# Order of strands in the first mixers from an estimate of VectorE's and ScalarE's queues

## The chip, the core and the metric

The kernel runs on one core of a Trainium2 chip. The core has a TensorE (PE in the profile; PEld is its weight load), a VectorE (DVE), a ScalarE (ACT), a GpSimd (POOL) and a SyncE (SP), which here only issues transfers. Each engine works through its own instruction stream in order and waits on semaphores for the others. The metric is the device time of one execution in microseconds.

## The reference

Two transformer blocks on one sequence of 256 tokens of width 1024, in fp32.

```
first_block:   xn = rms_norm(x); proj = xn @ w_in            # 1024 -> 2048 + 1792 columns
               ret = silu(g) * head_norm(retention(rotary(q), rotary(k), v))   # 4 heads of 128
               rw  = rwkv7_time_mix(rest of proj)            # 8 heads of 64, a state updated token by token
               h = x + concat(ret, rw) @ w_out
               h = h + hier_moe(rms_norm(h))                 # 32 experts, top 2
second_block:  moba and differential attention, w_out_2, then a PEER layer of 16384 experts
```

The change touches only the part from `proj` to `concat(ret, rw) @ w_out`: the first mixers.

## The kernel before

The first mixers are `phase_a` (L369). Weights come in units of 128 x 1024 fp32 and are multiplied with three products of reduced-precision parts. `ahead` (L190) makes the parts: a raw unit is loaded from SP's queue (L204, four raw buffers), ScalarE rounds it to a first part (`high`, L211), VectorE subtracts to get the second part (`low`, L218, three buffers), and only then is the next raw unit's load written (`load`). Each `next(ws)` hands out one unit and writes the first part three units and the second part two units ahead of its use. `mm3` (L294) multiplies first x first, first x second, second x first.

Thirty of the units are the input projection's (fourteen feature tiles, which are transposed, of 24 matmuls of 256 columns, and four token-major tiles of four units), eight are the output projection's. `features` (L488) and `feature_tile` (L512) compute the input projection. After a feature tile's matmuls VectorE makes three operations of 256 columns (`fe`, `d`, `ft`, L525 to L529).

All work of the first mixers is cut into strands, Python generators: `row_scales`, four `rwkv` (L563, each a pair of heads, in chunks of 64 tokens), two `ret_turn`, `retention`, two `ret_heads`, `out_weights`, `first_experts` (which starts the load of the expert weights into memory given back by the mixers), `features`, `project_out`. A strand writes some matmuls and the VectorE, ScalarE and GpSimd work on their results, and yields either a condition or a number: the planner's microseconds until its next matmuls should be written. `interleave` (L266) keeps one clock, `self.pe`, which each matmul advances by its columns; it always runs the first strand in the list that is ready, and if none is, sets the clock to the earliest wait. `features` yields 0.0, so it is ready whenever its condition holds. What a strand's answers cost on VectorE or ScalarE is in no clock: it is in the written numbers only.

Some of the numbers in an `rwkv` strand: 2.5 ahead of the products with `sq` and `rk`, 5.0 ahead of those with `bd` and `kd` (made by six VectorE operations, one a reciprocal, L637 to L646), 1.0 and 1.2 between the five levels of `X`, `Z`, `XT` (L707, L715, L716), 1.75 between the chunk states `Sb` (L745), 5.5 from the normalisation (L755 to L762, with two GpSimd steps between) to the last transposes.

Of the kernel before, what the change touches and what calls it, by code (L numbers as in the profile page):

```python
# [10 lines left out]
F32 = mybir.dt.float32  # L11
F32R = mybir.dt.float32r
# [3 lines left out]
AF = mybir.ActivationFunctionType  # L16
OP = mybir.AluOpType
# [142 lines left out]
    return o  # L160


class K:
    def __init__(self, ctx, tc, ins, out, dbg=None):
        self.ctx, self.tc, self.nc, self.i, self.out, self.dbg = ctx, tc, tc.nc, ins, out, dbg or {}
        self.n = 0
        self.pe = 0.0
        self.ps = ctx.enter_context(tc.tile_pool(name="ps", bufs=8, space=PSUM))
        self.cp = ctx.enter_context(tc.tile_pool(name="cp", bufs=1))
        self.hip = ctx.enter_context(tc.tile_pool(name="hip", bufs=4))  # L170
        self.raw = ctx.enter_context(tc.tile_pool(name="raw", bufs=RAW))
        self.lop = ctx.enter_context(tc.tile_pool(name="lop", bufs=LOP))
        self.hx = ExitStack()
        self.early = ExitStack()
# [15 lines left out]
    def ahead(self, srcs, depth=RAW):  # L190


        nc = self.nc
        srcs = iter(srcs)
        loaded, first, parts = deque(), deque(), deque()

        def load():
            s = next(srcs, None)
            if s is not None:
                if callable(s):  # L200
                    loaded.append(s)
                    return
                loaded.append(self.unit(self.raw))
                nc.sync.dma_start(loaded[-1], s)  # L204

        def high():
            if loaded:
                r = loaded.popleft()
                r = r() if callable(r) else r
                hi = self.unit(self.hip, F32R)  # L210
                nc.scalar.activation(hi, r, AF.Copy)  # L211
                first.append((hi, r))

        def low():
            if first:
                hi, r = first.popleft()
                lo = self.unit(self.lop, F32R)
                nc.vector.tensor_tensor(lo, r, hi.bitcast(F32), OP.subtract)  # L218
                parts.append((hi, lo))
                load()  # L220

        for _ in range(depth):
            load()
        yield
        high()
        yield
        low()
        high()
        yield
        low()  # L230
        high()
        yield
        while parts:
            high()
            low()
            yield parts.popleft()

    @staticmethod
    def halves(chunks):
# [22 lines left out]
    def tr(self, out, x):  # L262
        self.pe += 0.06
        self.nc.tensor.transpose(out, x, self.ident)  # L264

    def interleave(self, gens):  # L266

        wait = [0.0] * len(gens)  # L270
        live = dict(enumerate(gens))
        cond = {}
        while live:
            for n in list(cond):
                if cond[n]():
                    del cond[n]
                    wait[n] = self.pe
            ready = [n for n in live if n not in cond and wait[n] <= self.pe]
            if not ready:
                n = min((n for n in live if n not in cond), key=lambda n: wait[n])  # L280
                self.pe = max(self.pe, wait[n])
                ready = [n]
            n = ready[0]
            try:
                d = next(live[n])
            except StopIteration:
                del live[n]
                continue
            if callable(d):
                cond[n] = d  # L290
            else:
                wait[n] = self.pe + d

    def mm3(self, out, lh, rh, start, stop):  # L294
        mm = self.mm
        mm(out, lh[0], rh[0], start=start, stop=False)
        mm(out, lh[0], rh[1], start=False, stop=False)
        mm(out, lh[1], rh[0], start=False, stop=stop)
# [70 lines left out]
    def phase_a(self):  # L369
        nc, tc, i = self.nc, self.tc, self.i  # L370
        with ExitStack() as cx:

            early, even, self.bx = ExitStack(), ExitStack(), ExitStack()
            self.ap = {n: {"first": early, "even": even}.get(n, cx).enter_context(
                           tc.tile_pool(name=f"a_{n}", bufs=1, side="right" if n == "even" else "left"))
                       for n in ("even", "odd", "mid", "end", "xt", "tiny", "late", "first")}
            T = lambda pool, shape, tag, dt=F32, **k: self.t(self.ap[pool], shape, dt, tag, **k)
            lora, gup = (T("first", [128, 512], tag) for tag in ("lora", "gup"))
            nc.gpsimd.dma_start(lora, i["lora"])
            nc.gpsimd.dma_start(gup, i["gup"])  # L380
            rot = T("mid", [128, 2, 2, 64], "rot")
            nc.gpsimd.dma_start(rot, i["rot"])

            xt = [T("xt", [128, 8, S], f"xt{n}_", F32R) for n in range(2)]
            placed = deque()

            def out_weights():
                yield lambda: ("fm", 3) in self.done
                early.close()
                pw = cx.enter_context(tc.tile_pool(name="pw", bufs=1))  # L390
                for k in OUT_ORDER:
                    placed.append(self.t(pw, [128, D], F32, f"wo{k}_"))
                    nc.sync.dma_start(placed[-1], i["wO"][0, k])

            def first_experts():
                yield lambda: ("out", 2) in self.done
                even.close()
                self.places.extend(self.new_place(2 if not n else 1, "right") for n in range(2))
                self.once = ExitStack()
                self.prefetch(self.once.enter_context(tc.tile_pool(name="once", bufs=2, side="right", reuse_waits="tile")))  # L400
                for _ in range(2):
                    self.prefetch()

            self.src = [i["wB"][j] for j in range(192)]
            self.wq = []
            self.places = deque()
            ws = self.ahead(chain(self.halves(i["wA"][j] for j in range(15)), (placed.popleft for k in range(8))))
            self.got, self.done, self.tile = {}, set(), 0
            rt = {"qT": T("late", [128, 2, 4, S], "qT"), "v": T("mid", [128, 2, 512], "vr"), "g": T("late", [128, 2, 512], "gr")}
            rt["rs"] = [self.row_rstd(self.ap["tiny"], self.h[:, t], rt["v" if t else "g"].rearrange("p t d -> p (t d)"), "rows") for t in range(2)]  # L410
            self.transposed([self.h[:, t] for t in range(2)], "norm1_gain", *xt, ws, WARM[1])
            nc.sync.dma_start(self.cst2, i["cst"][:, CST_KEPT:])
            nc.gpsimd.dma_start(self.wr, i["wr"])
            o = VEC["norm2_gain"][0]
            nc.gpsimd.tensor_tensor(self.wr, self.wr, self.vec[:, o:o + 8, None].to_broadcast([128, 8, 36]), OP.mult)
            nc.gpsimd.dma_start(self.br, i["br"].to_broadcast([128, 36]))
            zs = self.rwkv_setup()
            self.interleave([self.row_scales(zs, rt, rot)] + [self.rwkv(p, zs, lora, gup) for p in range(4)] +
                            [self.ret_turn(rot, rt, g) for g in range(2)] +
                            [self.retention(rt)] + [self.ret_heads(rt, n) for n in range(2)] +  # L420
                            [out_weights(), first_experts(), self.features(xt, zs, rt, ws),
                             self.project_out(ws, OUT_ORDER, lambda k: ("ret", k // 2) if k < 4 else ("all", k - 4))])
        self.dump("mixh", self.mix[:, 0].bitcast(F32))
        places = [self.new_place() for _ in PLACES]
        self.places.extendleft(places[n] for n in reversed(PLACES))
        for n in range(3, MR + 3):
            self.prefetch({9: self.raw, 15: self.hip, 16: self.hip}.get(n))
        self.dump("h1", self.h)
# [1441 lines left out]
```

## Time and profile before

| | |
|---|---|
| Median of three runs | 1636.73 us (1633.51 to 1638.0) |
| Profiled execution | 1633.89 us, of which the span 1632.1 us |
| PE busy | 1581.5 us (97%) |
| VectorE busy | 967.6 us (59%) |
| ScalarE busy | 654.9 us (40%) |
| GpSimd busy | 218.8 us (13%) |

Shares over the whole span mix stages with different limits. The first mixers are the first 230 us or so, then come the experts, then the second block. The rows below are read by stretch, by wait and by instruction in time. A busy PE is one with matmuls under way; their ends are modelled, so small pauses can hide in it.

### The profile page before, as it was taken

The numbers are of one execution on the slowest core, as the hardware profiler recorded it, in microseconds if no ns is written. First come the engines' busy times: TensorE is split into PE (matmuls) and PEld (weight loads), VectorE is DVE, ScalarE is ACT, GpSimd is POOL, SyncE is SP. The second block draws the span as 40 slices with busy tenths as digits, with TensorE's granted clock in tenths as the row PEclk, the third lists the DMA queues.
The fourth block names the chain that finished last, engine by engine and source line by source line (L and its number), as shares of the span: only waits on it lengthen the run. The fifth ranks groups of instructions, "written<-read, shape, count | busy, mean of one in ns | idle before, by whom it ended". The sixth has DMA issues, their size and how long they took to land.

```text
span 1632.1 us, 28041 instructions
## 1 busy us (share of the span) xinstructions
PE 1581.5 (97%) x11118; PEld 1217.2 (75%) x11118; DVE 967.6 (59%) x1845; ACT 654.9 (40%) x1171; POOL 218.8 (13%) x249
## 2 busy tenths in 40 slices
PE   8999999999999999899999999999999999999998
PEld 7888873443444334378799999999999888888887
DVE  6676561121212112289889997788999755555554
ACT  5333341211111111266655556555544444444443
POOL 3213020000000000174210000123444000000000
PEclk9999999999999999999999999999999999999999
DMA  6324699999999999853355556555555566666664
GB/s 204 105 66 142 228 353 391 405 414 420 419 419 419 420 419 420 345 181 117 98 197 167 188 178 194 162 164 168 162 164 166 169 193 193 193 193 193 194 193 156
DMA packets 84297, 390.61 MB, mean 239 GB/s; under 512 B 9632, under 2 KB 9776, under 8 KB 63424
## 3 DMA queue, kind: packets, MB, share of 16 engines
q1 hardware_dynamic: 83088, 384.45, 65.6%
q0 software_dynamic: 928, 3.25, 0.5%
q8 instruction: 90, 1.47, 0.4%
q10 hardware_dynamic: 144, 1.05, 0.2%
q14 instruction: 47, 0.39, 0.1%
HBM read 386.62 MB, written 2.10 MB: 238 GB/s over the span
## 4 chain that ended last, share of the span: by engine, by line
PE 53%; DVE 2%; POOL 2%; issue 1%; ACT 0%; ACTq 0%; DVEq 0%; POOLq 0%
PE b L252 53%; POOL rs_r L338 1%; DVE u L218 1%; PE b L264 1%; DVE g L1727 0%; POOL rs_m L336 0%; POOL y L1418 0%; POOL rs_r L1407 0%; DVE oh L1835 0%; ACT s L1451 0%; DVE h L469 0%; DVE u L1684 0%; DVE ss L1405 0%; DVE qz L1430 0%; DVE mx L1447 0%
## 5 line engine op out<-in xcount | busy, mean ns | idle before, releaser
L211 ACT ACTIVATE u<-u 128x1024 fp32r<-128x1024 f32 x334 | 354.1, 1061 | 388.2 <-PE b L252 366.2
L218 DVE TENSOR_TENSOR u<-u,u 128x1024 fp32r<-128x1024 f32 x334 | 412.5, 1236 | 150.1 <-PE b L252 114.5
L252 PE MATMUL b<-mix,u 128*128 128x256 f32 x3456 | 425.6, 281 | 0.0
L252 PEld LDWEIGHTS b<-mix,u 128*128 128x128 f32 x3456 | 411.1, 188 | 0.0
L252 PE MATMUL b<-u,oh 128*128 128x512 f32 x1536 | 350.3, 390 | 2.0 <-ACT oh L1667 2.0
L252 PEld LDWEIGHTS b<-u,oh 128*128 128x128 f32 x1536 | 289.3, 188 | 62.8 <-ACT oh L1667 2.2
L252 PE MATMUL b<-mr,u 128*64 128x512 f32 x944 | 232.3, 595 | 16.2 <-DMA mr<-in_wB 16.0
L252 PEld LDWEIGHTS b<-mr,u 128*64 128x64 f32 x944 | 74.5, 137 | 158.0 <-issue 120.7
L1130 DVE TENSOR_TENSOR hh<-hh,b 128x512 f32<-128x512 f32 x16 | 11.0, 688 | 230.2 <-PE b L252 230.2
L1711 POOL TENSOR_TENSOR g<-g,gelu 128x4 f32<-128x4 f32 (+43 forms) x87 | 94.2, 1083 | 355.2 <-ACT gelu L1710 348.2
L252 PE MATMUL b<-u,xt 128*128 128x512 f32 x480 | 123.4, 407 | 0.8 <-DVE u L218 0.8
L252 PE MATMUL b<-mr,hT 128*64 128x512 f32 x480 | 115.5, 596 | 3.6 <-DVEq L1194 1.8
L252 PEld LDWEIGHTS b<-u,xt 128*128 128x128 f32 x480 | 89.1, 191 | 21.5 <-DVE u L218 1.1
L1175 DVE SCALAR_TENSOR_TENSOR u<-b,sw,u 128x512 fp32r<-128x512 f32 x32 | 23.9, 750 | 127.8 <-ACT u L1174 127.8
L252 PEld LDWEIGHTS b<-mr,hT 128*64 128x64 f32 x480 | 35.6, 137 | 70.9 <-issue 63.3
L1155 ACT ACTIVATE hT<-b 128x512 f32<-128x512 f32 x16 | 9.6, 598 | 160.1 <-PE b L264 160.1
L1668 DVE TENSOR_TENSOR oh<-g,oh 128x512 fp32r<-128x512 f32 x64 | 44.3, 693 | 41.1 <-ACT oh L1667 41.0
L1174 ACT ACTIVATE u<-b,sw 128x512 fp32r<-128x512 f32 x32 | 21.9, 687 | 105.1 <-PE b L252 105.1
L1303 POOL MEMSET qz<- 128x2048 f32 x2 | 3.5, 1800 | 448.8 <-DVEq L1194 448.8
L1727 DVE TENSOR_TENSOR g<-g,b 128x252 f32<-128x252 f32 (+47 forms) x111 | 61.5, 592 | 0.0
L1835 DVE TENSOR_TENSOR oh<-oh,gw 128x512 f16<-128x512 f16 x128 | 54.6, 465 | 0.0
L1129 ACT ACTIVATE hh<-b 128x512 f32<-128x512 f32 x16 | 9.6, 597 | 99.3 <-PE b L252 99.3
(381 smaller groups left out, 1713.7 us busy)
## 6 DMA issues: line engine op xcount, KB each, us to landing
mr<-in_wB SPq DMA_DIRECT2D x160, 1024.0 KB, 15.2
u<-in_down SPq DMA_DIRECT2D x128, 512.0 KB, 3.7
u<-in_up SPq DMA_DIRECT2D x128, 512.0 KB, 4.3
mr<-in_wB SPq DMA_DIRECT2D x36, 512.0 KB, 15.0
u<-in_wA SPq DMA_DIRECT2D x30, 512.0 KB, 3.7
u<-in_wB SPq DMA_DIRECT2D x28, 512.0 KB, 14.4
u<-in_wC SPq DMA_DIRECT2D x24, 512.0 KB, 4.0
u<-in_wQ SPq DMA_DIRECT2D x16, 512.0 KB, 3.6
```

The costliest lines, as they stand in the source:

```text
L211: nc.scalar.activation(hi, r, AF.Copy)
L218: nc.vector.tensor_tensor(lo, r, hi.bitcast(F32), OP.subtract)
L252: self.nc.tensor.matmul(out, l, r, start=start, stop=stop, **k)
L264: self.nc.tensor.transpose(out, x, self.ident)
L338: nc.gpsimd.tensor_tensor(r, m, self.mhalf[:, :width], OP.pow)
L1130: nc.vector.tensor_tensor(self.hh, self.hh, bs[1], OP.mult)
L1174: nc.scalar.activation(yh[:, o], b, AF.Copy, scale=sw)
L1175: nc.vector.scalar_tensor_tensor(yl[:, o], b, sw, yh[:, o].bitcast(F32), op0=OP.mult, op1=OP.subtract)
L1668: nc.vector.tensor_tensor(lo, src, hi.bitcast(F32), OP.subtract)
L1711: nc.gpsimd.tensor_tensor(dst[:, 0:n], dst[:, 0:n], g[:, 0:n], OP.mult)
L1727: nc.vector.tensor_tensor(d, d, s, OP.mult)
L1835: self.nc.vector.tensor_tensor(w[:, :, part].rearrange("p t (k x) -> p t k x", x=2), o[:, :, 0].rearrange("p t (k x) -> p t k x", x=2), se ...
```

## The change

A class `Queues` stands in for the program object while the first mixers' strands are written. It hands back every VectorE, ScalarE and GpSimd call unchanged, and keeps an estimated end for each of these three queues: the later of its last end and 0.25 us after the planner's clock, plus a constant and a price per element. GpSimd's end is kept but not used for waits. After a strand's step that wrote VectorE or ScalarE work, the strand's wait becomes the later of its written number and the estimated end plus 0.1.

The second part of a weight unit is no longer written in its `low` call. It is put on a list of what is owed, and written when the estimated end of VectorE's queue lies behind the clock at a strand's turn, or when a second one becomes owed, or when no finished unit is left. The load of the next raw unit moves with it. Where the strands of the second block use the same functions, nothing changes.

```diff
+class Queues:
+    COST = {"vector": (0.07, 1.04e-3), "scalar": (0.125, 0.91e-3), "gpsimd": (0.45, 2.1e-3)}
...
+    def note(self, e, n):
+        a, b = self.COST[e]
+        self.end[e] = max(self.end[e], self.k.pe + 0.25) + a + b * n
+        if e != "gpsimd":
+            self.last = self.end[e]
...
         def low():
             if first:
                 hi, r = first.popleft()
-                lo = self.unit(self.lop, F32R)
-                nc.vector.tensor_tensor(lo, r, hi.bitcast(F32), OP.subtract)
-                parts.append((hi, lo))
-                load()
+
+                def second():
+                    lo = self.unit(self.lop, F32R)
+                    self.nc.vector.tensor_tensor(lo, r, hi.bitcast(F32), OP.subtract)
+                    parts.append((hi, lo))
+                    load()
+                self.owed.append(second)
+                self.pay(0 if not self.queues else 1)
...
-        while parts:
+        while parts or self.owed:
             high()
             low()
+            if not parts:
+                self.pay()
             yield parts.popleft()
+
+    def pay(self, n=0):
+        while len(self.owed) > n:
+            self.owed.popleft()()
...
+    def modelled(self, gens):
+        nc = self.nc
+        self.nc = self.queues = Queues(self)
+        self.interleave(gens)
+        self.nc, self.queues = nc, None
+        self.pay()
...
             n = ready[0]
+            qs = self.queues
+            if qs:
+                qs.last = 0.0
+                if self.owed and qs.end["vector"] <= self.pe:
+                    self.pay(len(self.owed) - 1)
+                    qs.last = 0.0
...
                 wait[n] = self.pe + d
+                if qs and qs.last:
+                    wait[n] = max(wait[n], qs.last + 0.1)
...
-            self.interleave([self.row_scales(zs, rt, rot)] + [self.rwkv(p, zs, lora, gup) for p in range(4)] +
+            self.modelled([self.row_scales(zs, rt, rot)] + [self.rwkv(p, zs, lora, gup) for p in range(4)] +
```

## Rows read from the trace of the kernel before

**Rows 1.** Busy time by stretch: span, then PE, PEld, DVE, ACT, POOL; granted clock; DMA share.

```profile
20.00:60.00 40.00, 38.13 (x431) 33.50 (x429) 37.17 (x74) 18.51 (x35) 9.34 (x13) 1.00 0.41 131
...
100.00:150.00 50.00, 46.00 (x630) 38.76 (x632) 39.77 (x85) 16.49 (x35) 10.38 (x13) 0.93 0.23 75
```

**Rows 2.** The same view, two stretches of the expert stage.

```profile
380.00:400.00 20.00, 19.81 (x103) 9.16 (x101) 5.56 (x11) 4.02 (x9) 0.00 (x0) 1.00 1.01 422
660.00:680.00 20.00, 17.00 (x80) 6.70 (x78) 3.39 (x7) 1.48 (x3) 0.00 (x0) 1.00 0.99 401
```

**Rows 3.** What PE waits for, 10 to 240 us: total us, times, longest us.

```profile
PE b L252 <- DVE Z L707: 3.4, 3, 2.6
PE b L252 <- issue: 2.3, 3, 1.7
PE b L252 <- DVE u L218: 1.7, 1, 1.7
PE b L252 <- DVE Sb L745: 1.4, 1, 1.4
```

**Rows 4.** PE's instructions in time: start, us, what; idle time before and its releaser.

```profile
13.93 2.18 PE L252 MATMUL b<-xt,u 128*128 128x256 f32 x16 [1.74 <-DVE u L218]
...
23.00 0.67 PE L252 MATMUL b<-gs,gup 128*128 128x256 f32 x2 [1.68 <-issue]
...
101.84 1.12 PE L252 MATMUL b<-XT,Z 64*64 64x64 f32 x16 [2.63 <-DVE Z L707]
...
121.14 0.33 PE L252 MATMUL b<-Sb,G 64*64 64x64 f32 x4 [1.43 <-DVE Sb L745]
...
137.30 0.33 PE L252 MATMUL b<-Z,XT 64*64 64x64 f32 x4 [0.60 <-DVE Z L707]
```

**Rows 5.** Busy time by stretch, columns as in rows 1, behind the longest wait.

```profile
101.00:109.00 8.00, 7.16 (x62) 6.42 (x63) 4.34 (x9) 2.34 (x4) 0.00 (x0) 0.57 0.40 133
```

**Rows 6.** Groups by line, first 240 us: count | busy, mean ns | idle before.

```profile
L218 DVE TENSOR_TENSOR u<-u,u 128x1024 fp32r<-128x1024 f32 x30 | 38.2, 1272 | 2.6 <-PE b L252 2.1 <-ACT u L211 0.5
L211 ACT ACTIVATE u<-u 128x1024 fp32r<-128x1024 f32 x30 | 31.6, 1058 | 21.4 <-PE b L252 18.7 <-ACT XT L716 1.7 <-DMA u<-in_wA 0.9
```

**Rows 7.** VectorE's instructions in time around 100 us, columns as in rows 4.

```profile
93.74 0.42 DVE L755 TENSOR_REDUCE s<-b 128x4 f32<-128x256 f32 x1 [0.99 <-PE b L252]
...
95.56 0.42 DVE L760 TENSOR_REDUCE s<-y 128x4 f32<-128x256 f32 x1 [0.73 <-POOL y L759]
97.43 0.43 DVE L762 TENSOR_TENSOR y<-y,rs_r 128x256 f32<-128x256 f32 x1 [1.45 <-POOL rs_r L338]
...
100.15 1.21 DVE L218 TENSOR_TENSOR u<-u,u 128x1024 fp32r<-128x1024 f32 x1
101.28 0.41 DVE L707 TENSOR_TENSOR Z<-b,cst 128x256 f32<-128x256 f32 x1
```

**Rows 8.** VectorE's instructions in time around 120 us.

```profile
115.95 1.22 DVE L218 TENSOR_TENSOR u<-u,u 128x1024 fp32r<-128x1024 f32 x1
...
117.54 1.75 DVE L638 RECIPROCAL ri<-ri 128x256 f32<-128x256 f32 x1
...
120.81 0.28 DVE L745 TENSOR_SCALAR Sb<-b,gam 128x64 f32<-128x64 f32 x1
```

**Rows 9.** Instructions of VectorE and PE in time, 31 to 40 us, and one at 113.

```profile
31.04 0.81 DVE L628 TENSOR_SCALAR k<-av,vec 128x256 f32<-128x256 f32 x1
32.75 1.71 DVE L218 TENSOR_TENSOR u<-u,u 128x1024 fp32r<-128x1024 f32 x1
32.89 0.70 PE L252 MATMUL b<-rk,cst 128*128 128x256 f32 x2 [0.15 <-DVE rk L631]
...
37.68 0.42 DVE L646 TENSOR_TENSOR bd<-kr,e 128x256 f32<-128x256 f32 x1
...
39.27 1.09 PE L252 MATMUL b<-ar,bd 64*64 64x128 f32 x16
...
113.21 0.34 DVE L628 TENSOR_SCALAR k<-av,vec 128x256 f32<-128x256 f32 x1
```

More of the change, by code (lines that the diff above doesn't have):

```diff
@@ L160, in layout, with __init__, __getattr__, noted @@
     return o
+class Counted:
+    def __init__(self, engine, note):
+        self.engine, self.note = engine, note
+    def __getattr__(self, name):
+        f = getattr(self.engine, name)
+        if name == "dma_start":
+            return f
+        def noted(*a, **k):
+            r = f(*a, **k)
+            n = 1
+            for x in (a[1] if name == "tensor_reduce" else a[0]).shape[1:]:
+                n *= x
+            self.note(n)
+            return r
+        return noted
+class Queues:
+    COST = {"vector": (0.07, 1.04e-3), "scalar": (0.125, 0.91e-3), "gpsimd": (0.45, 2.1e-3)}
+    def __init__(self, k):
+        self.k, self.nc = k, k.nc
+        self.end = {e: k.pe for e in self.COST}
+        self.last = 0.0
+        for e in self.COST:
+            setattr(self, e, Counted(getattr(k.nc, e), lambda n, e=e: self.note(e, n)))
+    def __getattr__(self, name):
+        return getattr(self.nc, name)
+    def note(self, e, n):
[3 more added lines that the diff above has]
+            self.last = self.end[e]
 class K:
@@ L167, in __init__ @@
         self.pe = 0.0
+        self.owed, self.queues = deque(), None
         self.ps = ctx.enter_context(tc.tile_pool(name="ps", bufs=8, space=PSUM))
@@ L210, in high @@
                 hi = self.unit(self.hip, F32R)
-                nc.scalar.activation(hi, r, AF.Copy)
+                self.nc.scalar.activation(hi, r, AF.Copy)
                 first.append((hi, r))
```

## The prediction

> **What bounds the kernel now.** I read the stages first. Until 230 us the kernel computes its first mixers, the only part that the change rewrites; PE is busy 38.13 of 40 us in the stretch that starts at 20 us and 46.00 of 50 in the one that starts at 100 [rows 1]. VectorE is busy 37.17 of 40 us in the first of them: it is a near second limit there, and a source of single late answers afterwards. Behind 240 us comes an expert stage in which the DMA engines are full, 1.01 at 380 us and 0.99 at 660 us [rows 2]; its buffers are parts of memory that the first mixers give back, so I take a shift of the first mixers as a shift of the whole, one for one. There is no second effect to look for behind 240 us.
>
> Next, the list of what PE waits for inside the first mixers [rows 3]: VectorE's Z 3.4 us in three waits, its Sb 1.4 us, its second part of a weight ("u L218") 1.7 us, and "issue" 2.3 us. The 1.7 us is one wait that ends at 13.93, before the strands' first answers [rows 4], and the 0.8 us for "sel" that the view also lists belongs to the expert stage. What is left is about 7.8 us: 3.4 + 2.3 + 1.4 and 0.7 in single waits of 0.1 to 0.3. The long ones are 1.68 at 23.00, 2.63 at 101.84, 1.43 at 121.14 and 0.60 at 137.30 [rows 4]. Behind the longest, between 101 and 109 us, the granted clock is 0.57 [rows 5]: nearly all of the stretch ran at 1.2 instead of 2.4 GHz. The low share is 2 x 0.43 = 0.86 of 8 us, 6.9 us, and half of it, 3.4 us, is work that full clock would have saved. So no order of the strands can bring more than about 7.8 + 3.4 = 11.2 us, 0.7%. A measurement of this kernel can tell about 0.3%, 4.9 us, from no change.
>
> **The change part by part.** *The second parts move.* Thirty weight units go through the subtraction at 1272 ns each and eight more through the same line [rows 6]. Nothing is added or removed: the same instruction is written later in VectorE's stream. It helps where it stood ahead of an answer PE waited for. At 100.15 a second part stands directly ahead of the Z at 101.28 [rows 7]: 1.13 us. At 115.95 one stands ahead of the chain with the reciprocal, ahead of the Sb at 120.81 [rows 8]: 1.2 us, of a wait of 1.43. Bounds for both together: 0, if the estimate calls the queue empty and pays anyway, to 4.1, if both waits go (2.63 + 1.43). For the first I take 1.1. The wait at 23.00 is for gs, made from the second feature tile; between these first tiles the estimate finds VectorE's queue empty and pays at once, so I leave it (bound: 1.2 saved).
>
> What could be late in its place is the second part itself: at most one unit, 24 matmuls or some 3 us later. From 14 us on PE never waits for one, with two finished units in hand; one stays in hand. I cost it at nothing; with VectorE behind as it is from 20 to 60 us, the cover could fail once or twice at 1.2 us each (bounds 0 to 3). The load of the next raw unit is written with the second part, so SP's issue also comes up to a unit later, and the weight loads, the output weights and the expert prefetch behind it on that queue move with it. ScalarE waited for a weight's landing 0.9 us in all [rows 6]; I cost it at nothing, with the raw units in hand as cover, and bounds 0 to 2 if that goes.
>
> *Strands come later.* After a step that writes VectorE or ScalarE work, a strand now stays away until the estimated end of that queue plus 0.1, if that is later than the wait written in the strand. It removes a wait only where the estimate knows what delays. At 101.84 it doesn't: four steps of one head group's normalisation run from 93.74 until the y at 97.43 ends at 97.86 [rows 7], 4.1 us, since two of them wait for POOL (the gaps before 95.56 and 97.43). The estimate charges four operations of 256 (0.07 + 0.00104 x 256 = 0.336 each) and a small one, 1.42 us: 2.7 us short, and GpSimd's queue sets no strand's wait. The strand that writes Z is still sent too early, and PE, in order, still stands for what the second part doesn't account for. At 121.14 the reciprocal lasts 1753 ns [rows 8] and is charged 336; six operations and a second part are known, so that wait should go almost entirely together with the moved second part: 1.4 in all. At 137.30, 0.4 of 0.60. The other waits, each of 0.1 to 0.4 us, I leave as they are. Bounds: 0 to 2.0 beyond the moved second parts.
>
> *The filler is held back too.* This is the price. The strand "features" was always ready and its matmuls filled every gap. Now the end of each transposed feature tile sets its wait: 0.25 + 3 x 0.336 + 0.1 = 1.36 us of planner's time even on an empty queue, and where no strand is ready the planner's clock jumps there. PE on the chip has no such pause: the next tile's matmuls don't depend on it. So the planner's clock runs ahead by up to 1.36 for each tile of 2.8 us, and every wait written as a number is spent in fewer real microseconds. One place: the product with rk is at 32.89, already late by 0.15; bd is written at 37.68 and ready at 38.10, PE takes it at 39.27 [rows 9], and the strand's written wait is 5.0. From the product's end (33.6) the answer takes 4.5; with one jump 3.6 real us are left, and PE stands 0.9; with two, 2.3. The wait of 2.5 ahead of rk, shortened once, costs up to 1.4. Two heads (the first and the third) go through this beside transposed tiles: bounds 0 to 2 x (2.3 + 1.4) = 7.4. I take 1.4, nearest to the row, where PE already stood 0.15 with no slack.
>
> A row speaks against the estimate's single price: VectorE's k takes 0.81 us at 31.04 beside a POOL operation and 0.34 at 113.21 without, and a second part 1.71 at 32.75 instead of 1.27 [rows 6, 9]. The Trainium skill (GPSIMD Engine Reference, its opening property table and Key points) says that GpSimd shares its SBUF interfaces with VectorE, with contention in a two-port mode or with two SBUF inputs. By that rule the estimate is short by another 0.5 us at each such pair, beside four reciprocals that it undercharges by 1.4; by one price for all it would be right there, and the sum below could be 0.5 us lower. The trace agrees with the rule.
>
> *The sum.* -1.1 (Z) - 1.4 (Sb, second part and order) - 0.4 (second Z) + 1.4 (waits shortened) = -1.5 us. The clock's 3.4 stays, because 1.5 of the 2.63 us stay. The profiled execution took 1633.89 us (span 1632.1 and 1.8 around it): 1632.4. The median of the three runs, 1636.73, lies 2.8 above it: 1635.2, as a forecast 1635.
>
> **The rivals.** *Faster, by all the waits.* The estimate need not be right, only right enough: if the second part's move and other filler close the wait at 101.84 entirely, the clock stays at 2.4 GHz too. 2.63 + 1.43 + 0.60 + 0.2 + 3.4 = 8.3, so 1628.4. For it: PE's long waits are all for VectorE, behind work the planner has just written. Against it: the POOL round trips that it doesn't know, and filler that is now itself held back.
>
> *Slower, by the planner's clock running ahead.* Place: the transposed tiles, 18 to 48 and 75 to 117 us, where PE hardly waits today and there is nothing to gain. Price: 7.4 as above, less the 2.9 gained; a stand of over 2 us there may also be followed by a low clock, as that of 2.63 us was and those of 1.68 and 1.7 were not, another 3.4. That is +4.5 to +7.9, 1641 to 1645, say 1643. It decides from the point where two tile ends fall into one written wait of 5.0. For it: bd is ready only 1.2 us before PE takes it. Against it: in VectorE's full stretch the queue's own estimate becomes the longer wait and holds the strand back rightly.
>
> *It does nothing.* The new waits take hold only where the queue is over about 0.5 us behind (a Z on an empty queue is estimated at 0.69 after its matmuls, and 1.2 is written). If that is rare, the order stays as it is: 1636.7. It lies in the forecast's case.
>
> **How the numbers follow.** Forecast, with no effect beyond 4.9 us (1631.8 to 1641.6): 0.38. Faster rival: 0.34, since all its waits are VectorE's. Slower rival: 0.28. The likeliest case's own range is 1632 to 1641. The range for 8 in 10 reaches to 1626, nearly the ceiling of 11.2, and up to 1645, where the slower rival ends. The chances of faster, same and slower by 0.3% are these three.
>
> **What would show it.** In the changed profile: the wait for Z near 100 us shorter by about 1 us but there, and behind it still a stretch of low clock; the wait for Sb near 121 gone; L218 no longer directly ahead of a Z that PE waits for; new waits of PE between 20 and 50 us for rk or bd. Wrong, if no low clock is left in the first 230 us, if PE waits for "u L218" more than twice, or if the expert stage's DMA doesn't follow the shift.

## The result: slower by 12.3 us

The changed kernel took 1649.09 us (median of 4 runs, 1646.13 to 1652.17) against 1636.76 (4 runs): a ratio of 1.0083, 95% interval 1.0069 to 1.0097. That is 12.3 us more, on the side of the slower rival, but beyond its price and outside the range of 1626 to 1645. The profiled execution took 1646.13 us, its span 1644.4.

The totals of the engines after, from the profile's page. They hardly moved, so nothing was added to the work:

```profile
PE 1583.0 (96%) x11118; PEld 1217.1 (74%) x11118; DVE 967.6 (59%) x1845; ACT 654.6 (40%) x1171; POOL 221.2 (13%) x249
```

By stretch (span, then PE, PEld, DVE, ACT, POOL; granted clock; DMA share), first one stretch of the kernel before, then the answers to [rows 1, 2, 5]:

```profile
150.00:180.00 30.00, 28.59 (x596) 24.76 (x593) 13.07 (x29) 9.99 (x22) 7.28 (x12) 1.00 0.73 265
```

```profile
20.00:60.00 40.00, 35.19 (x451) 32.17 (x450) 32.01 (x66) 17.30 (x35) 8.74 (x12) 1.00 0.38 118
...
100.00:150.00 50.00, 44.99 (x662) 39.30 (x659) 38.28 (x84) 16.10 (x34) 13.86 (x15) 1.00 0.20 65
150.00:180.00 30.00, 24.08 (x530) 20.57 (x526) 11.67 (x27) 8.74 (x20) 4.29 (x7) 0.98 0.72 262
...
101.00:109.00 8.00, 7.38 (x95) 6.62 (x94) 4.80 (x10) 3.69 (x8) 3.06 (x3) 1.00 0.05 17
178.00:184.00 6.00, 4.75 (x78) 4.39 (x79) 1.99 (x6) 1.32 (x3) 3.59 (x6) 0.72 0.95 338
380.00:400.00 20.00, 20.00 (x94) 7.21 (x91) 2.69 (x4) 1.97 (x3) 0.00 (x0) 1.00 1.02 420
660.00:680.00 20.00, 17.00 (x81) 6.31 (x81) 3.58 (x7) 2.85 (x5) 0.00 (x0) 1.00 1.02 418
```

PE is busy 2.9 us less from 20 to 60 us, and 4.5 less from 150 to 180. The low clock of [rows 5] is gone; a shorter one, 2 x 0.28 x 6 = 3.4 us, stands behind 178 us, where PE has just waited longest. DMA in the expert stage is as full as before. The first matmul behind the first mixers, the router's, shows the whole loss. PE's instructions in time (start, us, what), before and after:

```profile
230.12 3.66 PE L252 MATMUL b<-wr,u 128*128 128x36 f32 x32
```

```profile
242.51 3.66 PE L305 MATMUL b<-wr,u 128*128 128x36 f32 x32
```

It comes 12.39 us later, and the span grew by 12.3. What PE waited for from 20 to 240 us (total us, times, longest), the answer to [rows 3]; most VectorE, ScalarE and GpSimd calls of the strands now carry line L174, that of the wrapper:

```profile
PE b L305 <- DVE Z L174: 9.2, 7, 4.2
PE b L305 <- DVE bd L174: 3.6, 2, 1.8
PE b L305 <- issue: 1.9, 2, 1.5
PE b L305 <- DVE y L174: 1.2, 1, 1.2
PE b L305 <- DVE rk L174: 0.9, 1, 0.9
```

With smaller ones the list comes to 18.3 us, where the first mixers had 7.8. PE's places in time, the answers to [rows 4, 9]:

```profile
23.96 0.67 PE L305 MATMUL b<-gs,gup 128*128 128x256 f32 x2 [1.47 <-issue]
...
33.85 0.70 PE L305 MATMUL b<-rk,cst 128*128 128x256 f32 x2 [0.87 <-DVE rk L174]
34.20 3.21 PE L305 MATMUL b<-xt,u 128*128 128x256 f32 x24
39.21 1.09 PE L305 MATMUL b<-ar,bd 64*64 64x128 f32 x16 [1.80 <-DVE bd L174]
...
93.73 0.33 PE L305 MATMUL b<-Z,XT 64*64 64x64 f32 x4 [1.77 <-DVE Z L174]
...
103.83 0.68 PE L305 MATMUL b<-XT,Z 64*64 64x64 f32 x16 [0.62 <-DVE Z L174]
...
117.11 0.33 PE L305 MATMUL b<-Sb,G 64*64 64x64 f32 x4
...
122.45 1.09 PE L305 MATMUL b<-ar,bd 64*64 64x128 f32 x16 [1.82 <-DVE bd L174]
...
178.63 0.95 PE L305 MATMUL b<-XT,Z 64*64 64x64 f32 x16 [4.16 <-DVE Z L174]
```

At their old places the waits are gone or small: 2.63 became 0.62, and Sb's 1.43 is no wait at 117.11. But the 2.63 is not gained. It belonged to the last of the second pair's five levels; now PE stands 1.77 at that strand's third level (93.73), 0.36 at its fourth (99.08) and 0.62 at its last, 2.75 together. The 0.60 at 137.30, the first level of the third pair, is 1.09 at 135.93. New waits are those for bd, twice, for rk, and the longest, for the fourth pair's last Z at 178.63. VectorE and GpSimd ahead of it:

```profile
175.86 0.42 DVE L174 TENSOR_REDUCE s<-y 128x4 f32<-128x256 f32 x1 [0.72 <-POOL y L174]
...
176.65 1.04 POOL L174 TENSOR_TENSOR rs_r<-rs_m,mhalf 128x4 f32<-128x4 f32 x1
177.72 0.42 DVE L174 TENSOR_TENSOR y<-y,rs_r 128x256 f32<-128x256 f32 x1 [1.44 <-POOL rs_r L174]
178.06 0.42 DVE L174 TENSOR_TENSOR Z<-b,cst 128x256 f32<-128x256 f32 x1
```

These are the steps of [rows 7] at another pair of heads, the third: Z stands in VectorE's stream behind a y that waits 1.44 us for GpSimd, and PE stands behind Z. In the kernel before this Z came at 167.97, ahead of the third pair's normalisation at 173.06, and PE did not wait for it. The stand of 1.77 is behind the normalisation of [rows 7] itself, the first pair's:

```profile
92.16 0.42 DVE L174 TENSOR_TENSOR y<-y,rs_r 128x256 f32<-128x256 f32 x1 [1.45 <-POOL rs_r L174]
...
93.16 0.41 DVE L174 TENSOR_TENSOR Z<-b,cst 128x256 f32<-128x256 f32 x1
```

The account: the product with gs starts 0.96 us later (23.00 to 23.96). This isn't shown to be the change's: VectorE's and ScalarE's work stands in the same order up to there in both, and over the profiled executions of all twenty kernels of this document this product starts between 22.57 and 26.13, at 24.63 in one whose only edit comes behind 90 us (the split normalisation on the kernel before). From there to the router 11.4 us are lost. PE's waits grew from 6.1 to 16.8, by 10.7, and pauses too short for the list by 0.3. PE's busy time, for the same 2645 matmuls in both traces, grew by 0.4 (200.75 to 201.19), although low clock costs 1.7 less (3.4 us of it in place of the 6.9 of [rows 5], at half). So some 2.1 us lie inside PE's busy time, whose ends are modelled; their cause isn't shown.

### The profile page after: what moved, and what is told of

Read it like the earlier page. It is cut to its first block, busy times and chain, and to the rows that moved or that the text cites. A ratio compares the mean times of both kernels' runs of the same rounds, so it can differ in the third digit from the quotient of the medians.

```text
span 1644.4 us, 28035 instructions
## 1 busy us (share of the span) xinstructions
PE 1583.0 (96%) x11118; PEld 1217.1 (74%) x11118; DVE 967.6 (59%) x1845; ACT 654.6 (40%) x1171; POOL 221.2 (13%) x249
## 4 chain that ended last, share of the span: by engine, by line
PE 52%; DVE 3%; POOL 2%; issue 1%; ACT 0%; ACTq 0%; DVEq 0%; POOLq 0%
PE b L305 51%; DVE u L262 1%; POOL rs_r L407 1%; DVE g L1796 0%; DVE mx L1516 0%; PE b L317 0%; POOL rs_m L405 0%; DVE s L1511 0%; POOL y L1487 0%; POOL rs_r L1476 0%; DVE qz L1499 0%; DVE oh L1904 0%; ACT s L1520 0%; DVE mx L1517 0%; DVE h L538 0%
## 5 line engine op out<-in xcount | busy, mean ns | idle before, releaser
L253 ACT ACTIVATE u<-u 128x1024 fp32r<-128x1024 f32 x307 | 325.7, 1062 | 366.9 <-PE b L305 347.7
L262 DVE TENSOR_TENSOR u<-u,u 128x1024 fp32r<-128x1024 f32 x306 | 377.7, 1235 | 146.9 <-PE b L305 112.5
L305 PE MATMUL b<-xt,u 128*128 128x256 f32 x336 | 47.6, 294 | 2.1 <-DVE u L262 2.1
```

What stands on the lines that cost most here:

```text
L253: self.nc.scalar.activation(hi, r, AF.Copy)
L262: self.nc.vector.tensor_tensor(lo, r, hi.bitcast(F32), OP.subtract)
L305: self.nc.tensor.matmul(out, l, r, start=start, stop=stop, **k)
```

## The experiments

Theories, with the letters of the expectations: *held filler* (A: since `features` waits, the numbers written beside the transposed tiles run short, and the loss is at rk and bd), *blind estimate* (B: GpSimd's round trips and the reciprocal are missing in it), *late second parts* (C), and, as these failed, *a fitted order* (the written numbers fit one order, and any other costs). Each time stands against runs of the kernel before on the same chip.

**Taking the change apart.** Only the moved second parts: the strands' new waits are left out.

```diff
-                if qs and qs.last:
-                    wait[n] = max(wait[n], qs.last + 0.1)
```

> Only the second parts move; no strand's wait is set by a queue's end. If the late second parts are the cause (theory C), most of the 12.3 us stays: about 1645, with PE waiting for the second parts. If the cause is the held-back filler (A) or the unpriced GpSimd waits (B), both of which need the new waits, the time is that of before within 4 us: 1634 to 1639, PE's waits 8 to 10 us.

1640.72 us, ratio 1.0025 (1.0008 to 1.0042): +4.4. Here the second part itself is late. VectorE and PE in time:

```profile
40.98 1.22 DVE L174 TENSOR_TENSOR u<-u,u 128x1024 fp32r<-128x1024 f32 x1
...
42.25 2.07 PE L305 MATMUL b<-xt,u 128*128 128x256 f32 x8 [3.63 <-DVE u L174]
```

It is written behind a reciprocal (1.75 us at 36.01) and eight more operations, and 3.4 us of low clock follow.

Only the waits: second parts are written at once.

```diff
-                self.pay(0 if not self.queues else 1)
+                self.pay(0)
```

> Only the strands' waits follow the queues; the second parts stand where they stood before. A and B: about as slow as the whole change, 1645 to 1651, waits of PE for bd of about 2 us twice. C: back to 1637.

1658.93 us, 1.0126 (1.0105 to 1.0148): +22.7, far over the whole change. So the two parts don't add up (4.4 and 22.7, together 12.3). PE's waits, 25.6 us in all, of which:

```profile
PE b L305 <- DVE Z L174: 7.8, 5, 4.2
PE b L305 <- DVE bd L174: 4.0, 2, 3.0
```

The whole change, but "features" (place 12 in the list) is not held:

```diff
-                if qs and qs.last:
+                if qs and qs.last and n != 12:
```

> The whole change, but the strand features (the filler) keeps its written wait of 0.0. A: the planner's clock no longer runs ahead, the waits for bd (3.6 us), rk (0.9) and y (1.2) go: 6 us or more back, 1637 to 1643. B alone: the long waits for Z stay (9.2 us) and the time stays at 1646 to 1650. C: no change, 1649.

1639.11 us, 1.0016 (1.0003 to 1.0029): +2.8. Without the hold 9.5 of the 12.3 us are back. bd and y are gone from PE's list, rk is at 0.2, and Z is back at 2.9; the late second part of the first experiment is there instead:

```profile
PE b L305 <- DVE u L174: 4.8, 3, 3.0
PE b L305 <- DVE Z L174: 2.9, 2, 1.5
```

**Is it the hold's length?** The kernel before, with the last `yield 0.0` of `feature_tile` set to 1.36, 0.68 or 0.2:

```diff
-        yield 0.0
+        yield 1.36
```

> The kernel before with one number changed: features waits 1.36 of planner's time after each feature tile, as the estimate makes it do on an empty queue. A: slower by 3 to 7 us, 1640 to 1644, with waits for bd of 1 to 2 us near 37 and 120 us that the kernel before doesn't have. B or C: no change, within 3 us of 1637.

> The kernel before with features waiting 0.68 after each feature tile, half of the earlier 1.36 that cost 21 us. A, with every planner's pause coming back as a real one: 14 x 0.68 = 9.5, so 1644 to 1648. If what counts is one unlucky order and not the length of the hold: anything from 1635 to 1658.

> The kernel before with features waiting 0.2 after each feature tile, a wait that no VectorE queue needs: 14 x 0.2 = 2.8 us of planner's pauses at most. If the loss grows with the held time, +2 to +4, 1637 to 1641. If the written numbers fit one order and any other loses, +5 or more. If small shifts are harmless, no change.

1657.3 us, 1.013 (1.0108 to 1.0152), +21 for 1.36; 1649.21, 1.0077 (1.0052 to 1.0102), +14.4 for 0.68; 1648.83, 1.0067 (1.0048 to 1.0087), +11.8 for 0.2. A hold alone makes the kernel slower, and with 1.36 it brings both kinds of wait:

```profile
PE b L252 <- DVE Z L707: 12.3, 8, 4.2
PE b L252 <- DVE bd L646: 4.0, 2, 3.0
```

The two longest, 4.17 at 97.58 and 4.15 at 188.58, are for a Z behind a normalisation. But the loss doesn't follow the hold's length: fourteen holds of 0.2 are 2.8 us, and cost 11.8. With 0.2 PE waits for neither bd nor, but for 0.2 us, for rk; Z is the loss, in nine waits:

```profile
PE b L252 <- DVE Z L707: 9.5, 9, 2.4
...
PE b L252 <- DVE Sb L745: 2.3, 1, 2.3
```

and its longest one stands again behind the normalisation:

```profile
102.03 0.43 DVE L762 TENSOR_TENSOR y<-y,rs_r 128x256 f32<-128x256 f32 x1 [1.45 <-POOL rs_r L338]
102.37 0.42 DVE L707 TENSOR_TENSOR Z<-b,cst 128x256 f32<-128x256 f32 x1
102.93 0.34 PE L252 MATMUL b<-Z,XT 64*64 64x64 f32 x4 [2.37 <-DVE Z L707]
```

The change with longer numbers ahead of rk and bd tests the places named by held filler:

```diff
-        yield 2.5
+        yield 3.9
...
-        yield 5.0
+        yield 7.7
```

> The whole change with two written numbers of each head strand lengthened by one planner's pause and by two: 2.5 to 3.9 ahead of rk and 5.0 to 7.7 ahead of bd. If the planner's clock runs ahead of PE by its pauses, PE's waits for bd (3.6) and rk (0.9) go: 3 to 5 us back, 1643 to 1647. If those waits have another cause, they stay and so does the time, 1649.

1651.9 us, 1.0093 (1.0074 to 1.0113): +14.9, no gain over the change. The waits named by the theory did go, and others took their place:

```profile
PE b L305 <- DVE Z L174: 9.6, 9, 2.2
PE b L305 <- DVE Sb L174: 3.2, 1, 3.2
...
PE b L305 <- DVE bd L174: 0.7, 1, 0.7
```

So held filler, as the whole of the loss, fell.

**Is it the estimate?** With filler free and second parts at once:

```diff
-                if qs and qs.last:
+                if qs and qs.last and n != 12:
...
-                self.pay(0 if not self.queues else 1)
+                self.pay(0)
```

> Strands' waits follow the queues, but not that of features, and the second parts stand where they stood before. If the held-back filler (A) and the late second parts near 40 us (C) are the whole loss, neither is left: 1630 to 1637, PE's wait for second parts only that at 12 us. If the waits of the other strands cost too (B), 1640 or more, with long waits for Z.

1649.79 us, 1.0084 (1.0065 to 1.0102): +15.0. Z is at 13.0 us in eight waits. The same with the missing prices, 1.42 per reciprocal and 0.73 and 1.45 per normalisation, added to VectorE's estimated end:

```diff
+        self.idle(1.42)
         nc.vector.reciprocal(ri, ri)
...
+        self.idle(0.73)
         nc.vector.tensor_reduce(s2, y2, AX.X, OP.add)
         r = self.rstd(self.ap["end"], s2, 64, 4, RWKV_EPS)
+        self.idle(1.45)
```

> As the previous kernel, with VectorE's estimate lengthened by what the trace shows and the estimate leaves out: 1.42 for each reciprocal, 0.73 and 1.45 for the two waits on GpSimd in each normalisation. If the unpriced time (B) makes strands come too early, the waits of PE for Z and Sb (some 4 us) shrink and the time falls by 2 to 5 us against the previous kernel: 1627 to 1634. If it is of no account, within 2 us of it.

1641.73 us, 1.0046 (1.0027 to 1.0065): +6.9; Z falls from 13.0 to 2.1. That spoke for the blind estimate. Next, the change without held filler (+2.8 above), with second parts at once until tile 8 and late from there, and then the same with the prices:

```diff
-                self.pay(0 if not self.queues else 1)
+                self.pay(0 if not self.queues or self.tile < 8 else 1)
```

> The whole change, with features free as in the third run, and the second parts written at once until eight feature tiles are done. If late second parts near 40 us (a wait of 3.0 us and 3.4 us of low clock behind it) were what that run still lost, it gains 4 us on its 1639: 1632 to 1637, and PE's waits for second parts fall to the one at 12 us. If any new order costs about as much, 1637 to 1645.

> The previous kernel with the reciprocals and the GpSimd waits in VectorE's estimate. If the unpriced time still sends strands too early: 2 to 4 us faster than the previous one, 1629 to 1634, below the kernel before. If an order that is as good as the written one is all there is: 1633 to 1639.

1639.99 us, 1.0015 (1.0001 to 1.003), +3.0 without prices; 1659.45, 1.0126 (1.0107 to 1.0145), +22.5 with them. The prices that gave back 8 us in one order cost 19 in the other, where second parts come late:

```profile
PE b L305 <- DVE u L174: 10.7, 4, 3.2
```

A truer estimate is thus no cure by itself. The waits-only kernel with second parts that don't count in the wait of the strand that writes them:

```diff
+                    last = qs.last if qs else 0.0
                     self.nc.vector.tensor_tensor(lo, r, hi.bitcast(F32), OP.subtract)
+                    if qs:
+                        qs.last = last
```

> As the run with the waits alone (1658.9), the second parts early, but their 1.1 us no longer set the wait of the strand that writes them. If the second parts made that run worse than the whole change by holding the filler longer, the time falls to that of the whole change, 1646 to 1651. If they made it worse by standing in front of other answers on VectorE, it stays at 1656 to 1661.

1660.1 us, 1.0146 (1.0119 to 1.0172): +25.3, with the same waits as without the edit, and VectorE's work in the same order until 228 us: the charge set hardly any wait. It isn't why early parts and waits go badly together.

**A neutral shift.** The kernel before with the planner's price of a transposition, or the constant of a matmul's, about a third higher: no estimate, no hold, no moved part.

```diff
-        self.pe += 0.06
+        self.pe += 0.08
```

> The kernel before with one price of the planner's clock changed: 0.08 for a transpose instead of 0.06. No hold, no estimate. If the written numbers fit one order and a small shift of the strands against each other loses it: 1641 to 1652, with more than 5 us of waits for Z. If only a held filler loses: 1634 to 1639.

```diff
-... + 0.01) * (1 if m > 64 else 0.5)
+... + 0.013) * (1 if m > 64 else 0.5)
```

> The kernel before with another price changed: 0.013 for a matmul's start instead of 0.010. A second shift without hold or estimate. Fitted order: 1641 to 1652 with waits for Z of over 5 us; only a held filler loses: 1634 to 1639.

1644.65 us, 1.0043 (1.0027 to 1.0059), +8.2; and 1644.31, 1.0051 (1.0034 to 1.0067), +7.9. PE's longest groups with the first edit, then the second:

```profile
PE b L252 <- DVE Sb L745: 3.7, 2, 2.3
...
PE b L252 <- DVE u L218: 2.1, 2, 1.2
```

```profile
PE b L252 <- DVE Z L707: 9.9, 9, 2.8
```

Two unrelated small shifts cost two thirds of what the change costs, at the same operations: Sb and second parts, or Z.

**The normalisation.** The strand gives up its turn at each GpSimd step, so that the operations that wait for GpSimd are written later:

```diff
+        yield 1.6
         nc.vector.tensor_reduce(s2, y2, AX.X, OP.add)
         r = self.rstd(self.ap["end"], s2, 64, 4, RWKV_EPS)
+        yield 2.3
         nc.vector.tensor_tensor(y, y, r[:, :, None].to_broadcast([128, 4, 64]), OP.mult)
-        yield 5.5
+        yield 1.6
```

On the change:

> The whole change, with the normalisation of each head written in three steps (waits 1.6, 2.3 and 1.6 in place of 5.5), so that VectorE is not blocked in order while GpSimd works. If Z behind these waits is the main loss, PE's waits for Z fall from 9.2 to under 5 us and the time by 4 us or more: 1640 to 1645. If the loss has another cause: 1647 or more.

1642.79 us, 1.0041 (1.0027 to 1.0056): +6.4, some 6 us less than the change. Around the wait of 4.16:

```profile
171.43 0.41 DVE L174 TENSOR_TENSOR Z<-b,cst 128x256 f32<-128x256 f32 x1
171.99 0.68 PE L305 MATMUL b<-XT,Z 64*64 64x64 f32 x16 [1.14 <-DVE Z L174]
...
175.18 0.42 DVE L174 TENSOR_TENSOR y<-y,rs_r 128x256 f32<-128x256 f32 x1 [2.36 <-POOL rs_r L174]
```

Z now goes ahead of the y that waits for GpSimd, and PE stands 1.14 us. The 1.77 is 0.62, and no low clock is left behind 20 us. Z's sum is 6.2 in place of 9.2, bd's 2.4 in place of 3.6. On the kernel before, and on the two filler-free kernels at +3.0 (second parts late from tile 8) and +2.8 (late throughout):

> The kernel before with the same three steps. Its longest wait for Z, 2.63 us with 6.8 us of low clock behind it, stands behind such a normalisation. If that is what it loses: 1629 to 1634. If any shift loses more than this saves: 1639 or more, with other waits for Z.

> Features free, the second parts at once until eight tiles are done, and the normalisation in three steps. If the three causes found are the whole loss and the rest of the estimate helps: 1629 to 1634, faster than the kernel before, no wait for Z above 1.5 us. If a new order as such costs some 7 us, as the two price changes did: 1637 to 1645.

> The same without the exception for the first eight tiles. The wait of 3 us for a second part near 40 us and 3.4 us of low clock behind it come back: 3 to 5 us slower than the previous kernel. If they don't matter here, within 2 us of it.

1643.33 us, 1.0043 (1.0029 to 1.0057), +6.9; 1650.22, 1.0077 (1.0059 to 1.0094), +12.6; 1652.76, 1.0095 (1.0078 to 1.0112), +15.2. The edit that helped the change costs the others 7 to 12 us. In the kernel before, the 2.63 is gone, but PE stands 2.65 us for a Z behind the fourth pair's chain with the reciprocal (145.46) and 2.79 for a normalised y, now written late (209.86). The change and all eighteen experiments are slower than the kernel before, by 2.8 to 25.3 us.

## Why the prediction was wrong, by its own steps

*What bounds the kernel.* The ceiling on the gain was not tested, as nothing was gained. The shift of the later stages is one for one: 12.39 us at the router, 12.3 in the span. Wrong as a list: the argument treated the 7.8 us of before as all there was to lose, and "The other waits, each of 0.1 to 0.4 us, I leave as they are." In the changed order they didn't stay.

*The second parts move, strands come later.* The -1.4 for Sb is right. The -1.1 for Z did not come: 2.0 of the 2.63 went at its place, and 2.1 came back at the two levels before, 1.77 of it behind the same normalisation. The -0.4 for the second Z did not either; that wait grew by 0.5. "The clock's 3.4 stays" was wrong in its place and size: the clock from 101 to 109 us is 1.00, and the low clock behind 178 us costs 1.7. The late second part, taken at nothing, costs nothing in the changed kernel from 20 us on, since u is not in PE's list there; but its cover is thin. As soon as the filler isn't held, or the strands' waits are left out, PE waits 3.0 to 3.6 us for it at one place.

*The filler is held back.* The places were right: rk 0.87 at 33.85, bd 1.80 at 39.21 and 1.82 at 122.45. At 39.21 the cause can be read as it was argued:

```profile
38.63 0.42 DVE L174 TENSOR_TENSOR bd<-kr,e 128x256 f32<-128x256 f32 x1
```

From the end of the product with rk (34.55) bd's answer takes until 39.05 us, 4.5 as before, while the filler between the two ends at 37.41, 2.9 us after that product, for a written wait of 5.0; before, PE came for bd 5.7 us after the product [rows 9]. The stand of 1.80 lies between the forecast 0.9 of one jump and 2.3 of two. Together, less the old 0.15, these waits are 4.3 us: "I take 1.4" was too small by 2.9, inside its bounds of 0 to 7.4.

*The step that failed* is that this price was put at 1.4 us and sought only at rk and bd, "where PE already stood 0.15 with no slack". There it is 4.3. Taking the hold away gives 9.5 us, and lengthening just those two numbers gives none. The larger share of the new waits is Z, which went from 3.4 to 9.2 us. The 4.16 alone is more than bd's 3.6; it stands behind the third pair's normalisation, which held up no Z before. The prediction knew the 2.7 us by which its estimate falls short of a normalisation, and used them only to explain why an old wait would stay, not as a hazard for every Z that a new order writes behind one. The split on the change supports this: the 4.16 and the 1.77 shrink by 4.2 together, the low clock's 1.7 goes, and the time falls by some 6 us. As the split also changes the order, its whole gain isn't theirs alone: bd's waits shrink too, and 1.4 of the 6.0 us between the two profiled executions lie ahead of the product with gs, where both kernels are alike.

*The slower rival* had the side, the held filler and some of the places, at 1641 to 1645. Its price left out Z, its places (18 to 48 and 75 to 117 us) leave out the longest wait, at 178.63, and the 3.4 us that it added for low clock did not come on top: all low clock behind 20 us costs 1.7, less than before. *The signs* of being wrong all stayed away: some low clock is left, PE waits once for a second part (2.1 us, ahead of 14 us), and the expert stage's DMA follows the shift. They guarded the gains, and the loss came by another way.

Two neutral shifts cost 8 us. So up to two thirds of the 12.3 may be what this kernel pays for any order to which its written numbers were not fitted. That isn't shown: the shift is another order than the change's, and some orders cost only 3 us. How the 12.3 divides between the hold, the blind estimate and such a misfit stays open, as edits change the order and don't add up, and so does why late second parts give back about 10 us when the strands' waits are on (22.7 to 12.3).

*The single price.* The row that spoke against it came again: VectorE's k takes 0.81 us at 32.00 beside GpSimd's operation at 31.97, and 0.35 at 115.52 without one.

```profile
32.00 0.81 DVE L174 TENSOR_SCALAR k<-av,vec 128x256 f32<-128x256 f32 x1
...
115.52 0.35 DVE L174 TENSOR_SCALAR k<-av,vec 128x256 f32<-128x256 f32 x1
```

By the Trainium skill (GPSIMD Engine Reference, Key points) the two engines share SBUF interfaces; the trace agrees. It is a small term beside the waits.

## What to carry to other kernels

Where an order is held together by numbers fitted by hand, the waits of the old profile bound the gain of a new order and say nothing of its losses: list the operations that can block an in-order queue (here VectorE's, with its waits for GpSimd, its reciprocal, its second parts) and ask what a new order could put behind each. A wait that is gone at its old place may stand one or two steps earlier, as the 2.63 did, so compare by strand and not by place. Before a scheduling idea is tried, shift the order by something neutral: if that costs 8 us, a planned gain of 1.5 will drown in it. A truer estimate does not pay by itself: the same prices gave back 8 us in one order and cost 19 in another. Whether it pays with numbers fitted to it was not tried.

## What the runs showed that was not expected

- A GpSimd round trip in VectorE's stream costs little by itself (0.72 and 1.44 us), but PE, which needed the Z written behind it, stood 4.16 us: two such waits and the operations between them lay ahead of that Z.
- Over the profiled executions of all twenty kernels, the span follows PE's waits from 20 to 240 us (without the router's own, for sel) and the share of low clock from 10 to 240 us, counted as lost time, together (correlation 0.96; waits alone 0.90).
- PE's clock in the first 20 us differs between kernels that begin alike: 1.00 before, 0.83 after. The start of the product with gs does not simply follow it: it is 25.40 with the changed price of a transposition, whose clock there is 1.00 too.

```profile
0.00:20.00 20.00, 14.19 (x84) 13.27 (x84) 9.16 (x20) 11.16 (x20) 7.38 (x20) 1.00 0.79 261
```

```profile
0.00:20.00 20.00, 14.09 (x72) 13.02 (x73) 8.60 (x19) 11.10 (x19) 7.92 (x20) 0.83 0.78 261
```
